# A two-layer decoder trunk: PE's instructions of both attentions tied to the order of the source

## The chip, the core and the metric

The kernel runs on one core of a Trainium2 chip. The metric is the time of one execution on the device in microseconds (us); of several executions the median is taken. Engines are named as in the profile: PE is TensorE (matmuls; PEld its weight loads), DVE is VectorE, ACT is ScalarE, POOL is GpSimd, SP is SyncE, whose queue issues nearly all DMAs.

## The reference

One sequence of 512 tokens, width 1024, float32. Two layers: a "forgetting" attention (FoX: 16 heads of 64, causal softmax with an added term from a running sum of log-sigmoid gates), then a latent attention (MLA: 8 heads, 128 plain and 64 rotary dimensions, keys and values from one shared compressed stream). Each is followed by an output projection, a residual and a squared-ReLU MLP with 4096 hidden units.

```python
def reference(x, ...):
    for layer in range(DEPTH):                      # DEPTH = 2
        h = rms_norm(x, norm_mix_g[layer])
        if layer < N_A_LAYERS:                      # layer 0
            x = x + fox_mixer(h, fox_w_in[layer], fox_b_f[layer], fox_w_out[layer])
        else:                                       # layer 1
            x = x + mla_mixer(h, ..., k_nope, k_rope, v_shared, cos, sin)
        x = x + sq_relu_mlp(rms_norm(x, norm_ffn_g[layer]), ffn_w_up[layer], ffn_w_down[layer])
        if layer == N_A_LAYERS - 1:
            k_nope, k_rope, v_shared = mla_shared_kv(x, ...)
    return rms_norm(x, final_norm_g)

# inside both mixers, for each block of 128 queries:
        logits = jnp.where(kpos[None, :] <= qpos[:, None], logits, -jnp.inf)
        p = jax.nn.softmax(logits, axis=-1).astype(v.dtype)
        return jnp.einsum('bhqk,bkhd->bqhd', p, v)
```

## The kernel before

Every product of float32 matrices is made of three matmuls on rounded operands: a tensor is split into a high half (ACT casts it) and a low half (DVE subtracts the high half from the source), and `three` issues high x high, high x low, low x high into one PSUM bank. Split tiles of 128 x 512 have the tag "r" (40 buffers). Weights arrive as pieces (tag "raw", two buffers; halves "whi" and "wlo", three buffers); a piece is loaded and split when the one before it is asked for. The weight pieces of the output projections numbered 3 and 4 go into "r" tiles instead.

**An attention** (`attention`, lines 378 to 412) runs over pairs of heads and, within a pair, over the four query blocks from the last (i = 3, 512 keys) to the first (i = 0, 128 keys). Step n of its loop does, in this order in the source:

1. `start(p)` on the first block of a pair: the filling is run until this pair's projections have been issued.
2. `scores` for both heads into two "sc" banks. In FoX that is six matmuls with a contraction of 64, alternating between the two heads, which lie in the upper and the lower 64 partitions. In MLA each head has three matmuls over 128, and then come six over 64, alternating.
3. `soft_step`: DVE adds the bias and takes the row's extreme, ACT takes the exponential, DVE normalizes.
4. For the block of three steps earlier (SKEW = 3): `turn` for each head. PE transposes the probabilities into a "tp" bank (three banks), ACT casts them to "pth" (high), DVE subtracts to "ptl" (low).
5. After a pair's last block, in between: `values` for each head (PE, from "pth" and "ptl" into a "tp" bank), and ACT and DVE combine the result to the context. In FoX ACT copies one half and DVE adds the other.
6. `fill.run`: a set number of matmuls of other work. In FoX it is 12 a step, and 18 more after the first head's values; in MLA 6 and 6. The work is a list of generators: in FoX the query and key projections of pairs 1 to 7 (24 matmuls each, "acc" banks) with two value projections, and then the first three columns of the output projection (`out_begin`), as far as contexts are there; in `out_begin` a context is split when first used (`ctx_part`). In MLA it is the query, key and value projections of later pairs, then the output projection. Two more columns, in the "sc" banks, are added as "out2" when the scores are over.

**What sets the order of instructions.** Each engine runs its instructions in the order of its stream, with semaphores between engines. The order within a stream is not the source's by itself: the scheduler of the kernel language plays the program through ahead of time, and lets an engine take, of the instructions that are ready in that play, the one written first. An instruction written earlier but not ready is passed. A tile waits for a free buffer of its tag.

The class `Engine` (lines 101 to 124) wraps PE, DVE, ACT and SP. While `order["on"]` is set, it adds from each instruction to the one before it on the same engine an edge without a semaphore, so that the stream keeps the order of the source. Before the change this is on only in the two MLP stages (`ffn`, lines 873 to 878), whose order is written out by hand as a list of steps: for PE, DVE and ACT, and for SP in the steps below 9. In both attentions the scheduler is free.

The pairs of FoX are numbered 0 to 7, its steps 0 to 31 and a tail of four without scores; pair p's first scores are in step 4p. Pair p's values come in step 4p + 7.

Of the kernel before, what the change touches and what calls it, by code (L numbers as in the profile page):

```python
# [95 lines left out]
@with_exitstack  # L96
def trunk(ctx: ExitStack, tc: tile.TileContext, xT, wts, gains, fing, rope, out):
    real = tc.nc
    order = {"on": False, "loads": False, "last": {}}

    class Engine:

# [4 lines left out]
        def __getattr__(self, op):  # L107
            fn = getattr(self.engine, op)

            def call(*args, **kw):  # L110
                ins = fn(*args, **kw)  # L111
                if order["on"] and (self.name != "sync" or order["loads"]):
                    before = order["last"].get(self.name)
                    if before is not None:
                        tc.add_manual_dep(
                            ins.ins,
                            before,
                            mybir.DependencyInfo(mybir.DependencyClass.NoSync, mybir.DependencyReason.DATA),
                            reason="as written",
                        )  # L120
                    order["last"][self.name] = ins.ins.name
                return ins

            return call

    class Core:
        tensor, vector, scalar, sync = (Engine(n) for n in ("tensor", "vector", "scalar", "sync"))
# [23 lines left out]
    def nm(s):  # L151
        uid[0] += 1
        return f"{s}{uid[0]}"
# [197 lines left out]
    def soft_step(scs, n, biases):  # L351
        m, rs, r = (small.tile([P, 2], F32, tag=f"sm{j}", name=nm("sm"), bufs=4) for j in range(3))
        Ls = [tt(), tt()]
        for e in range(2):

            nc.vector.tensor_tensor_reduce(
                out=Ls[e][:, :n], in0=scs[e][:, :n], in1=biases[e], scale=-1.0, scalar=3.4e38, op0=ALU.add, op1=ALU.min, accum_out=m[:, e : e + 1]
            )
        for e in range(2):
            nc.scalar.activation(  # L360
                out=Ls[e][:, :n], in_=Ls[e][:, :n], func=AF.Exp, scale=-1.0, bias=m[:, e : e + 1], accum_out=rs[:, e : e + 1]
            )
        nc.vector.reciprocal(r, rs)
        for e in range(2):
            nc.vector.tensor_scalar_mul(Ls[e][:, :n], Ls[e][:, :n], r[:, e : e + 1])
        return Ls

    def turn_unit(L, i, pth, ptl):

        n = (i + 1) * P  # L370
        tp = bank("tp")
        for j in range(i + 1):
            nc.tensor.transpose(tp[:, j * P : (j + 1) * P], L[:, j * P : (j + 1) * P], ident)
        src = tp[:, :n].rearrange("p (j q) -> p j q", q=P)
        nc.scalar.copy(pth[:, i : 4 * i + 1 : 3, :], src)
        nc.vector.tensor_tensor(ptl[:, i : 4 * i + 1 : 3, :], src, f32(pth[:, i : 4 * i + 1 : 3, :]), op=ALU.subtract)

    def attention(pairs, apool, start, scores, values, fill, per_step, out_gen):


        bufs = {}

        def turn(st, e):
            p, i, Ls = st
            if (p, e) not in bufs:
                bufs[p, e] = [apool.tile([P, 13, P], F32R, tag=t, name=nm(t), bufs=3) for t in ("pth", "ptl")]
            turn_unit(Ls[e], i, *bufs[p, e])

        steps = [(p, i) for p in range(pairs) for i in range(NB - 1, -1, -1)]
        ready = {}  # L390
        for n in range(len(steps) + SKEW + 1):
            if n < len(steps):
                p, i = steps[n]
                if i == NB - 1:
                    start(p)
                ready[n] = (p, i, soft_step(*scores(p, i)))
            elif n == len(steps):
                fill.add("out2", out_gen(["sc"] * 2))
            m = n - SKEW
            st = ready.pop(m, None)  # L400
            done = (m - 1) // NB if m > 0 and m % NB == 0 else None
            if done is not None:
                values(done, 0, *bufs.pop((done, 0)))
            if st:
                turn(st, 0)
            if done is not None:
                fill.run(per_step[1] if n < len(steps) else 6)
                values(done, 1, *bufs.pop((done, 1)))
            if st:
                turn(st, 1)  # L410
            if n < len(steps):
                fill.run(per_step[0])

    def out_begin(name, tags, outs, ready, part):

        mine = [(bank(t), blocks(piece(name))) for t in tags]
        outs += mine
        for ks in ((0, 2), (2, 4), (4, 6), (6, 7)):
            for pp, w in mine:
                for k in range(*ks):  # L420
                    while ready() <= k:
                        yield 1000
                    three(pp, *w[k], *part(k), k == 0, False)
                yield 3 * (ks[1] - ks[0])
# [3 lines left out]
    with ExitStack() as fx:  # L428
# [111 lines left out]
        def start(p):  # L540
            if p:
                fill.until(("qk", p))
            for q in (p, p + 1):
                if q < FH // 2 and q not in nbs:

                    nb = apool.tile([P, 2, S], F32, tag="nb", name=nm("nb"))
                    nc.sync.dma_start(nb, csc[2 * q : 2 * q + 2, :].partition_broadcast(P))
                    nbs[q] = nb

        def scores(p, i):  # L550
            n = (i + 1) * P
            q = slice(i * P, n)
            (qh, ql), (kh, kl) = qk[p]
            scs = [bank("sc"), bank("sc")]
            for a, b2, st, sp in ((qh, kh, True, False), (qh, kl, False, False), (ql, kh, False, True)):
                for e in range(2):
                    rows = slice(e * FHD, (e + 1) * FHD)
                    mm(scs[e][:, :n], a[rows, q], b2[rows, :n], start=st, stop=sp)
            nb = nbs[p]
            mask = maskz[:, S - P :].unsqueeze(1).to_broadcast([P, 2, P])  # L560
            nc.vector.tensor_tensor(nb[:, :, q], nb[:, :, q], mask, op=ALU.add)
            return scs, n, [nb[:, e, :n] for e in range(2)]

        def values(p, e, pth, ptl):
            if p >= 4:
                fill.until(("v4", 2 + (p - 4) // 2))
            if e == 0:
                ctxs.append(rt())
            cs = f32(ctxs[p])
            hd = 2 * p + e  # L570
            cx = bank("tp")
            for j in range(NB):
                w = v2[hd // 4, j][:, hd % 4].rearrange("p a d -> p (a d)")
                mm(cx[:, j * P :], w, pth[:, 4 * j : 3 * j + 4, :], start=j == 0, stop=False)
                mm(cx[:, j * P :], w, ptl[:, 4 * j : 3 * j + 4, :], start=False, stop=j == NB - 1)
            own = slice(e * FHD, (e + 1) * FHD)
            oth = slice((1 - e) * FHD, (2 - e) * FHD)
            nc.scalar.copy(cs[own], cx[oth])
            nc.vector.tensor_tensor(cs[own], cs[own], cx[own], op=ALU.add)
            whole[0] += e  # L580
# [21 lines left out]
        def out_gen(tags):  # L602
            return out_begin("fo", tags, outs, lambda: whole[0], ctx_part)

        fill.add("out", out_gen(["acc"] * 3))
        fill.run(12)
        attention(FH // 2, apool, start, scores, values, fill, FILL1, out_gen)
        fill.until("out2")
        split_ctx(FH // 2 - 1)
# [22 lines left out]
    def ffn(acc, layer, tokens, tail, begin):  # L632
# [8 lines left out]
        with ExitStack() as fs:  # L641
# [229 lines left out]
            begin(at)  # L871
            tail(len(seq), max(posted.values()), at, locals())
            for step in sorted(due):
                order["on"], order["loads"] = True, step < 9
                for _, _, fn, args in sorted(due[step], key=lambda d: d[:2]):
                    fn(*args)
            order["on"] = False
            order["last"].clear()
        state["next"] = first + [n for n, _ in PIECES].count(gname)

# [23 lines left out]
    def by_features(e, after, at, fn):  # L904
# [53 lines left out]
        for j, part in enumerate(("u2", "u3", "c11", "c21", "v", "c12", "u4", "c22")):  # L958
            for b in range(2):
                at(e + j // 2, 4, combine, b, part)  # L960

    ffn(acc, 0, ytok, by_features, put_away)
    for f in range(4, KD):
        close_feature(f)
# [11 lines left out]
    with ExitStack() as mx:  # L976
# [150 lines left out]
        cq = normed(q_t, rstd_tile(rs), "qa")  # L1127
        fill.until("q0")
        attention(MH // 2, apool, lambda p: fill.until(f"q{p}"), scores, values, fill, FILL2, out_gen)
        fill.until("out2")  # L1130

# [50 lines left out]
    def by_tokens(e, after, at, fn):  # L1182
# [44 lines left out]
        for j, part in enumerate(("u2", "u3", "c11", "c21", "v", "c12", "u4", "c22")):  # L1227
            for b in range(2):
                at(e + j // 2, 4, combine, b, part)

    ffn(acc, 1, xtok, by_tokens, turn_stream)
    psum["stack"].close()
    assert state["next"] == len(PIECES)
# [107 lines left out]
```

## Time and profile before

| | |
|---|---|
| median of 3 runs | 1143.74 us (1143.55 to 1149.49) |
| profiled execution, its own time | 1149.94 us |
| its span, first to last instruction | 1148.2 us |
| mean clock granted to PE | 0.99 |
| instructions | 14285, of these 5356 matmuls on PE |
| FoX attention, first scores to last values | about 52 to 234 us |
| MLA attention, first scores to last values | about 669 to 766 us |

A row in order of time reads: start, duration, engine, line, operation, output tile <- input tiles (buffer numbers left out), shape, count of instructions merged, and in brackets the idle time of the engine before it with what ended it. Every wrapped instruction has the line of the wrapper, L111, so rows are told apart by their tiles: "sc <- r" scores, "tp <- ident" turns, "tp <- pth, v" or "pth, r" values, "acc <- r, whi" projections. A merged row's duration runs to its last end; matmuls overlap in the records, so distances are taken from start to start. In the rows by stretches the columns are: from and to, length, then busy time and count of PE, PEld, DVE, ACT and POOL, then the clock granted to PE as a share of full speed, the DMA engines' share and GB/s.

### The profile page before, as it was taken

Reading aid. Unit: us, or ns where it says so; the run is one execution under the profiler, and the core shown is the slowest. Engines: PE = TensorE matmul, PEld = TensorE weight load, DVE = VectorE, ACT = ScalarE, POOL = GpSimd, SP = SyncE. Lnnn points to the kernel's source line nnn. Section 1 sums busy time; section 2 is a strip of 40 time slices with the busy share of each in tenths; the row PEclk is TensorE's granted clock in tenths of the full one; section 3 lists DMA queues with packets and bytes.
Section 4 is the critical chain, followed back from the end, with each engine's and each line's share of the span. In section 5 each row is a group of like instructions: output and inputs, shape, how many; then the busy total and the mean of one; then the engine's idle time right before and its main releaser. Section 6 shows DMA issues by size and latency. Waiting matters only on the chain.

```text
span 1148.2 us, 14285 instructions
## 1 busy us (share of the span) xinstructions
PE 1125.5 (98%) x5356; PEld 919.2 (80%) x5356; DVE 782.2 (68%) x1401; ACT 577.2 (50%) x1057; POOL 19.8 (2%) x83
## 2 busy tenths in 40 slices
PE   8999999999999999999999899999999999999996
PEld 6777887788888888888887768788888888888885
DVE  6797888863567676668793678846356666765785
ACT  5565655653664445434353456635555544444612
POOL 1000000001000000000000100000100000000000
PEclk9999999999999999999999889999999999999998
DMA  5322222142915215221343121222351522511301
GB/s 186 130 95 89 75 77 88 38 157 83 324 43 184 74 55 183 74 66 55 127 157 100 35 65 52 90 76 92 127 204 55 183 64 66 186 60 48 129 1 74
DMA packets 36822, 116.66 MB, mean 102 GB/s; under 512 B 4224, under 2 KB 4864, under 8 KB 36752
## 3 DMA queue, kind: packets, MB, share of 16 engines
q1 hardware_dynamic: 35888, 114.15, 29.9%
q10 hardware_dynamic: 864, 1.60, 0.4%
q8 instruction: 42, 0.69, 0.3%
q14 instruction: 28, 0.23, 0.1%
HBM read 109.40 MB, written 6.32 MB: 101 GB/s over the span
## 4 chain that ended last, share of the span: by engine, by line
PE 94%; DVE 2%; ACT 1%; DMA 1%; issue 1%; POOL 0%; ACTq 0%; SPq 0%
PE up L111 34%; PE acc L111 21%; PE go L111 17%; PE sc L111 8%; PE tp L111 7%; PE keep L111 6%; DVE r L111 1%; ACT t L111 1%; DVE fs L111 1%; DMA nb<-csc 0%; DMA t<-xT 0%; DVE wlo L111 0%; DVE t L111 0%; ACT whi L111 0%; ACT r L111 0%
## 5 line engine op out<-in xcount | busy, mean ns | idle before, releaser
L111 PE MATMUL acc<-r,whi 128*128 128x512 f32 x600 | 196.4, 408 | 5.4 <-ACT whi L111 4.9
L111 PE MATMUL up<-r,r 128*128 128x512 f32 x808 | 192.6, 390 | 0.0
L111 PEld LDWEIGHTS up<-r,r 128*128 128x128 f32 x808 | 151.2, 188 | 31.5
L111 PE MATMUL up<-r,whi 128*128 128x512 f32 x544 | 171.0, 391 | 0.0
L111 DVE TENSOR_TENSOR wlo<-raw,whi 128x1024 fp32r<-128x1024 f32 (+3 forms) x95 | 111.2, 1171 | 51.9 <-ACT whi L111 50.9
L111 DVE TENSOR_TENSOR t<-s,t 128x512 fp32r<-128x512 f32 x84 | 57.8, 688 | 121.8 <-ACT t L111 121.7
L111 ACT CAST whi<-raw 128x1024 fp32r<-128x1024 f32 (+3 forms) x95 | 95.5, 1008 | 88.2 <-PE acc L111 34.2
L111 PEld LDWEIGHTS acc<-r,whi 128*128 128x128 f32 x600 | 111.0, 192 | 31.6 <-ACT whi L111 4.9
L111 ACT ACTIVATE s<-up 128x512 f32<-128x512 f32 x56 | 33.4, 597 | 190.7 <-PE up L111 190.7
L111 PE MATMUL acc<-r,wlo 128*128 128x512 f32 x300 | 119.3, 398 | 0.0
L111 PEld LDWEIGHTS up<-r,whi 128*128 128x128 f32 x544 | 101.8, 188 | 21.0
L111 PE MATMUL up<-r,wlo 128*128 128x512 f32 x288 | 112.3, 390 | 0.0
L111 PE MATMUL go<-r,t 128*128 128x512 f32 x360 | 86.5, 389 | 0.0
L111 PE MATMUL sc<-r,r 128*128 128x512 f32 (+6 forms) x480 | 81.8, 360 | 2.1 <-ACT r L111 1.7
L111 PEld LDWEIGHTS go<-r,t 128*128 128x128 f32 x360 | 67.6, 188 | 14.0
L111 PE MATMUL go<-whi,t 128*128 128x512 f32 x240 | 78.8, 389 | 0.0
L111 PEld LDWEIGHTS sc<-r,r 64*128 64x128 f32 (+1 forms) x480 | 56.0, 188 | 26.1 <-issue 9.2
L111 ACT ACTIVATE t<-t,sm 128x512 f32<-128x512 f32 (+3 forms) x96 | 53.3, 557 | 36.7 <-DVE sm L111 36.5
L111 PEld LDWEIGHTS acc<-r,wlo 128*128 128x128 f32 x300 | 57.4, 191 | 12.9 <-issue 0.4
L111 PEld LDWEIGHTS up<-r,wlo 128*128 128x128 f32 x288 | 54.1, 188 | 11.5
L111 DVE TENSOR_TENSOR r<-raw,r 128x512 fp32r<-128x512 f32 x72 | 46.5, 684 | 22.1 <-ACT r L111 22.1
L111 DVE TENSOR_TENSOR r<-q,r 128x512 fp32r<-128x512 f32 x94 | 60.4, 683 | 0.0
(182 smaller groups left out, 1866.1 us busy)
## 6 DMA issues: line engine op xcount, KB each, us to landing
raw<-wts SPq DMA_DIRECT2D x122, 512.0 KB, 3.6
q<-wts SPq DMA_DIRECT2D x56, 512.0 KB, 4.6
nb<-csc SPq DMA_DIRECT2D x8, 512.0 KB, 4.7
t<-xT SPq DMA_DIRECT2D x8, 256.0 KB, 6.4
r<-xT SPq DMA_DIRECT2D x8, 256.0 KB, 6.3
xmid<-r SPq DMA_DIRECT2D x8, 256.0 KB, 7.3
r<-xmid SPq DMA_DIRECT2D x8, 256.0 KB, 4.2
xkeep<-r SPq DMA_DIRECT2D x8, 256.0 KB, 2.7
```

Source lines behind the costliest of these rows:

```text
L111: ins = fn(*args, **kw)
```

## The change

While the loop of an attention is issued, the wrapper now ties PE's instructions to the order of the source: scores, values and turns, and filling, as in the list above. `order["on"]` becomes a tuple of engine names instead of a flag. In the MLP stages the tuple names the engines that the flags named before. DVE, ACT, SP and POOL stay free in the attentions, and no instruction is added, removed or changed. The order begins with the first PE instruction of the loop and ends with its last; what lies before and behind is not tied to it.

```diff
-    order = {"on": False, "loads": False, "last": {}}
+    order = {"on": (), "last": {}}
...
                 ins = fn(*args, **kw)
-                if order["on"] and (self.name != "sync" or order["loads"]):
+                if self.name in order["on"]:
...
+        order["on"] = ("tensor",)
         steps = [(p, i) for p in range(pairs) for i in range(NB - 1, -1, -1)]
         ready = {}
         for n in range(len(steps) + SKEW + 1):
...
             if n < len(steps):
                 fill.run(per_step[0])
+        order["on"] = ()
+        order["last"].clear()
...
             for step in sorted(due):
-                order["on"], order["loads"] = True, step < 9
+                order["on"] = ("tensor", "vector", "scalar") + ("sync",) * (step < 9)
                 for _, _, fn, args in sorted(due[step], key=lambda d: d[:2]):
                     fn(*args)
-            order["on"] = False
+            order["on"] = ()
             order["last"].clear()
```

## The prediction

> **What bounds the kernel now.** I read the page's first part and its chain, then the busy time by stretches, then TensorE (PE), ScalarE (ACT) and VectorE (DVE) in order of time at the places where PE's order in the trace leaves the order of the source.
>
> ```profile
> PE 1125.5 (98%) x5356; PEld 919.2 (80%) x5356; DVE 782.2 (68%) x1401; ACT 577.2 (50%) x1057; POOL 19.8 (2%) x83
> PE 94%; DVE 2%; ACT 1%; DMA 1%; issue 1%; POOL 0%; ACTq 0%; SPq 0%
> ```
>
> ```profile
> 52.30:180.90 128.60, 128.60 (x792) 105.77 (x791) 105.60 (x291) 75.62 (x182) 0.00 (x0) 1.00 0.27 92
> 180.90:262.00 81.10, 79.60 (x401) 62.34 (x401) 61.77 (x139) 45.60 (x98) 0.00 (x0) 1.00 0.26 85
> ```
>
> PE is the bound: a microsecond that it loses ends up in the time. The first stretch is the first attention up to the scores of pair 6: PE is busy all of it (columns: length, busy time and count of PE, PEld, DVE, ACT, POOL, clock granted, DMA). A regular step there looks like this:
>
> ```profile
> 90.76 0.97 PE L111 MATMUL sc<-r,r 64*128 64x512 f32 x6
> 91.66 0.87 PE L111 MATMUL tp<-ident,t 128*128 128x128 f32 x6
> ...
> 94.45 0.62 PE L111 MATMUL acc<-r,whi 128*128 128x512 f32 x2
> 94.91 0.39 PE L111 MATMUL acc<-r,wlo 128*128 128x512 f32 x1
> 95.22 0.80 PE L111 MATMUL sc<-r,r 64*128 64x384 f32 x6
> ```
>
> Six score matmuls (three for each head), six turns, twelve of filling: exactly lines 391 to 412. The step takes 95.22 - 90.76 = 4.46 us, one filling matmul (94.91 - 94.45) / 2 = 0.23, and the one before a change of kind 0.31, so a change costs about 0.1. So the order asked for is already there, in 806 matmuls in a row by my walk through the loop. It is left only near 184, 201 to 216 and 225 to 232 us, and in the second attention, beyond a few single matmuls, near 737 to 745 and 759 to 766. There the old order put ready work into the time of a wait. The change's cost is what each wait is without that cover.
>
> **The change part by part.** No instruction is added or removed, and ACT, DVE, SP and POOL get no new order; their streams can only follow PE's. In the MLP stages the tuple names the same engines as the old flags, so nothing changes there: 0. In the 806 matmuls nothing moves: 0, and there is no cover to lose.
>
> *Place A, pair 6's first scores (step 24).* The source has only six filling matmuls between the last of pair 6's key projection and its scores.
>
> ```profile
> 184.10 0.38 PE L111 MATMUL tp<-ident,t 128*128 128x128 f32 x2
> 184.85 0.50 PE L111 MATMUL sc<-r,r 64*128 64x512 f32 x2 [0.36 <-ACT r L111]
> 186.33 0.73 PE L111 MATMUL sc<-r,r 64*128 64x512 f32 x4
> 189.48 0.79 PE L111 MATMUL sc<-r,r 64*128 64x384 f32 x6
> ```
>
> ```profile
> 184.18 0.62 ACT L111 CAST r<-t 128x512 fp32r<-128x512 f32 x1 [0.41 <-DVE t L111]
> ```
>
> ```profile
> 185.19 0.69 DVE L111 TENSOR_TENSOR r<-t,r 128x512 fp32r<-128x512 f32 x1
> ```
>
> The keys' high half is ready at 184.80 and the low half at 185.88. As written, PE runs the first score pair at 184.85, waits until about 185.95, runs two pairs (0.57), six turns (0.63) and the filling (2.93, the rest of the 4.46): next scores at 190.1 against 189.48, **+0.6**. The least is 4.46 + 0.1 from 184.10 without a wait, -0.8.
>
> *Place B, the turn to the output projection (steps 27, 28).* Behind the last projection matmul (200.89) the source has twelve matmuls of the output projection, then values, turn, twelve more, then pair 7's scores. The trace skips the twelve.
>
> ```profile
> 200.89 0.40 PE L111 MATMUL tp<-pth,v 128*128 128x512 f32 x1
> 206.00 0.44 PE L111 MATMUL tp<-ident,t 128*128 128x128 f32 x2 [0.90 <-DVE ptl L111]
> 207.20 0.78 PE L111 MATMUL sc<-r,r 64*128 64x384 f32 x3
> 215.64 0.79 PE L111 MATMUL sc<-r,r 64*128 64x384 f32 x3
> ```
>
> ```profile
> 203.07 0.62 ACT L111 CAST r<-raw 128x512 fp32r<-128x512 f32 x1
> 205.51 0.62 ACT L111 CAST r<-r 128x512 fp32r<-128x512 f32 x1
> ```
>
> ```profile
> 203.09 0.68 DVE L111 TENSOR_TENSOR r<-t,r 128x512 fp32r<-128x512 f32 x1
> 207.06 0.69 DVE L111 TENSOR_TENSOR r<-r,r 128x512 fp32r<-128x512 f32 x1
> ```
>
> The twelve need the splits of contexts 0 and 1 (r<-r). Those contexts are old, yet they are split only at 205.5: tiles tagged "r" come in written order here, the key's low half (DVE 203.09), then a weight piece in two halves (ACT 203.07 on), then the contexts. I take this order to stay. Without values and turn in between: key low half until 203.77, DVE's two weight halves until 205.15, ACT's first context cast from the second one's start, 204.46 to 205.08. PE waits 200.89 to 205.1 (4.2 us), and 0.5 more for the low halves (DVE at about 205.9 and 206.5). Behind it wait values, turn and pair 7's scores; their softmax has until pair 7's turns, some 10 us later, so nothing else becomes late. Against that stand the old order's idle 0.90, the heads' 384-column scores run apart (0.72 each time, where six together take 0.73), and ten changes of kind, 1.0: together 2.6. **+2.1**; least, if the splits come early, -2.6.
>
> *Place C, the last pair (steps 31 to 35).* Behind the values of pair 6 the source has nine output matmuls that need that very context, then six turns of pair 7 (twelve matmuls) in three buffers, then values.
>
> ```profile
> 225.31 1.03 PE L111 MATMUL tp<-ident,t 128*128 128x128 f32 x7
> 227.64 0.97 PE L111 MATMUL acc<-r,whi 128*128 128x512 f32 x3
> 233.67 1.29 PE L111 MATMUL sc<-r,r 128*128 128x512 f32 x4
> ```
>
> ```profile
> 225.51 0.58 ACT L111 COPY r<-tp 64x512 f32<-64x512 f32 x1 [0.49 <-PE tp L111]
> 226.96 0.63 ACT L111 CAST r<-r 128x512 fp32r<-128x512 f32 x1
> ```
>
> ```profile
> 226.12 0.69 DVE L111 TENSOR_TENSOR r<-r,tp 64x512 f32<-64x512 f32 x1 [0.37 <-ACT r L111]
> 227.91 0.68 DVE L111 TENSOR_TENSOR r<-r,r 128x512 fp32r<-128x512 f32 x1
> ```
>
> Copy, add, cast, subtract: the first of the nine can't start before about 227.5, the second before 228.2. As written PE idles from 225.7, where its four turns end, to 227.5 and again 0.6, and the nine end at 230.1. Three turns (0.8 us) fill the buffers; each next one waits for an ACT cast of about 0.5 and a DVE subtraction of 0.55 or less, so the last subtraction for head 0 ends near 233.3. Values (1.35), six score-bank matmuls (1.4) and values (1.35) end at 237.5, against 233.67 with the same work done: **+3.8**. The old order had put three of the turns and the six matmuls into the first wait. Without waits -0.4.
>
> *Place D, second attention, pair 3's first scores.* The third matmul needs a query half from DVE:
>
> ```profile
> 738.22 1.28 DVE L111 TENSOR_TENSOR r<-acc,r 128x512 fp32r<-128x512 f32 x2
> ```
>
> PE waits about 1.1 us to 738.9, then runs undivided pairs; the walk gives 746.7 against 747.06 at the next but one step: **-0.3** (bounds -1.4 with no wait, and +0.8 when the saving is absent).
>
> *Place E, its last turns.* Seven filling matmuls stood between the turns, the first and the last of them here:
>
> ```profile
> 759.61 0.70 PE L111 MATMUL acc<-r,whi 128*128 128x512 f32 x2
> 761.60 0.47 PE L111 MATMUL acc<-r,whi 128*128 128x512 f32 x1
> 761.92 0.47 PE L111 MATMUL tp<-pth,r 128*128 128x512 f32 x1
> ```
>
> Values can't start earlier (three buffers and DVE, as in C), so 7 x 0.23 = 1.6 comes behind, less some changes of kind: **+1.3** (0 to 1.6).
>
> Sum of the places: 0.6 + 2.1 + 3.8 - 0.3 + 1.3 = **+7.5 us**.
>
> **The clock.** Idle PE has a second price here.
>
> ```profile
> 640.49:650.73 10.24, 9.13 (x26) 7.50 (x27) 4.40 (x10) 2.56 (x5) 2.36 (x12) 0.50 0.00 1
> 667.80:671.21 3.41, 2.11 (x7) 1.07 (x7) 3.05 (x5) 3.31 (x7) 0.00 (x0) 1.00 0.35 115
> 671.21:678.04 6.83, 6.83 (x17) 4.42 (x16) 4.95 (x11) 2.65 (x7) 0.00 (x0) 0.50 0.29 77
> 203.59:207.00 3.41, 2.34 (x13) 1.28 (x12) 3.32 (x6) 3.01 (x8) 0.00 (x0) 1.00 0.52 159
> ```
>
> Behind a 3.41 us stretch in which PE was busy 62% the granted clock was 0.50 for 6.83 us; behind one with 69% it stayed at 1.00; the other fall lasted 10.24 us. At half clock 6.83 us do the work of 3.4, 10.24 that of 5.1. B has 4.2 us of no work at all; C has 2.4 idle in the 2.6 us from 225.7, and 2 more in the turns. I take a fall of the short kind at each, **+6.8**, and none at E (about 2 us idle, in short pieces): ends 0 and three long ones, 15.4. The Trainium skill, "TensorE: Matmul & The Clock Gate", section "HAM oscillation", warns of idle gaps over about 3.4 us. By that rule B falls and C does not; the trace speaks against it, for in the stretch of 62% PE was idle 1.3 us in all.
>
> Total +7.5 + 6.8 = +14.3 us. The profiled execution took 1149.94 (span 1148.2), which gives 1164.2; the median run is 6.2 us shorter, perhaps by a clock fall or two, and the same sum from 1143.74 gives **1158.0**.
>
> **The rivals.**
> 1. *Order pays, faster.* The splits of contexts 0 and 1 run early, in ACT's idle time before 201, and C, D and E find their operands: -0.8 - 2.6 - 0.4 - 1.4 - 0 = -5.2, 1138.5, a few less if the fall at 671 goes too. It decides at B: the first split would have to be there by 200.9 instead of 205.5. Against it: C's chain of four operations, 2.7 us long, which no order of other engines shortens. Chance 0.08.
> 2. *The stalls, but a clock that holds*: +7.5, 1151.2. For it: the 69% stretch. Chance 0.13.
> 3. *One fall, at the wait longer than a stretch (B)*: +10.9, 1154.6. For it: only there is a whole stretch empty. Chance 0.13. This is also what the skill's rule above makes of it.
> 4. *Three falls, or long ones*: up to 7.5 + 15.4 = +22.9, 1166.6. Chance 0.14.
> 5. *B's splits come early, the rest as forecast*: 0.6 - 2.6 + 3.8 - 0.3 + 1.3 = +2.8, 1146.5. Chance 0.09.
> 6. *The change does next to nothing*, since the trace is in the written order for most of both attentions and the rest is made up: 1143.7. Against it: no PE slack behind 262 us. Chance 0.07.
>
> **How the numbers follow.** The forecast itself has 0.36. A difference under 0.5% (5.7 us) is about what a measurement of this kernel can't tell from none. Slower: forecast and rivals 2 to 4, 0.76; same: 5, 6 and part of 1, 0.19; faster: the rest of 1, 0.05. The range runs from rival 5's lower side, 1145, to rival 4, 1167; the forecast's own is 1153 to 1163.
>
> **What the profile after would show.** PE's matmuls in written order throughout, sc x6 undivided; idle of PE before an "acc" released by an "r" of ACT or DVE of about 4 us near 201 and 2 us near 226; turns of the last pairs apart by DVE's "ptl"; clock 0.50 behind the first two. It is wrong if "r<-r" is cast before 201, if the clock stays at 1.00, or if PE's time grows where the order was the same before.

## The result and the profile after

The changed kernel took 1153.62 us (median of 4, 1153.27 to 1156.18) beside 1143.70 for the kernel before, a ratio of 1.0082 with the 95% interval 1.0056 to 1.0109. Measured once more, on the chip of some of the experiments, the ratio was 1.0045 (1.0025 to 1.0065). So it is slower: by 9.9 us in the first measurement and by 5.2 in the second, where 14.3 was forecast. The profiled execution took 1153.33 us.

The page of the kernel after, with busy time, granted clock and chain, and below it the clock row of the kernel before:

```profile
span 1151.5 us, 14282 instructions
...
PE 1121.2 (97%) x5356; PEld 917.6 (80%) x5356; DVE 782.4 (68%) x1401; ACT 577.1 (50%) x1057; POOL 20.1 (2%) x83
...
PEclk9999999899999999999999899999999999999998
...
PE 91%; DVE 4%; ACT 2%; DMA 1%; issue 1%; POOL 1%; SPq 0%; ACTq 0%; DVEq 0%
```

```profile
PEclk9999999999999999999999889999999999999998
```

PE's share of the chain fell from 94% to 91%, DVE's and ACT's rose: PE now waits for them. The clock row has three 8s, as it had before, but the first of them is new: it stands in the eighth of the 40 slices, near 206 us. The stretches of the first attention (columns as before):

```profile
52.30:181.20 128.90, 128.90 (x793) 105.99 (x792) 105.76 (x291) 75.72 (x182) 0.00 (x0) 1.00 0.29 93
181.20:271.00 89.80, 81.74 (x401) 64.37 (x400) 62.17 (x138) 45.59 (x98) 0.00 (x0) 0.96 0.24 77
202.52:205.93 3.41, 0.50 (x1) 0.19 (x1) 3.26 (x6) 3.41 (x8) 0.00 (x0) 1.00 0.14 20
205.93:212.76 6.83, 6.17 (x15) 4.97 (x16) 3.02 (x6) 1.12 (x3) 0.00 (x0) 0.50 0.45 146
229.82:233.24 3.42, 1.84 (x14) 1.51 (x12) 3.01 (x7) 2.55 (x5) 0.00 (x0) 1.00 0.00 0
```

The first row is what it was to 0.3 us: where the order had been the written one, nothing moved. The loss is in the second row, 89.80 us where the same work took 81.10. The third and fourth are place B, a stretch in which PE was busy only 15% and the clock at half behind it; the fifth is place C, where PE was busy 54% and the clock held.

To give each place its share I read the time between four points that both kernels pass with the same work done: the first scores of pair 5 (step 20), of step 26 and of step 31, and the first matmul of the MLP. Rows of PE in order of time, before and after (the first row of each is cut short by the view's window; all six score matmuls start there):

```profile
160.95 0.73 PE L111 MATMUL sc<-r,r 64*128 64x512 f32 x4
...
193.55 0.62 PE L111 MATMUL sc<-r,r 64*128 64x256 f32 x6
...
221.81 0.55 PE L111 MATMUL sc<-r,r 64*128 64x128 f32 x6
...
261.79 0.39 PE L111 MATMUL up<-r,whi 128*128 128x512 f32 x1
```

```profile
161.22 0.50 PE L111 MATMUL sc<-r,r 64*128 64x512 f32 x2
...
194.51 0.62 PE L111 MATMUL sc<-r,r 64*128 64x256 f32 x6
...
227.40 0.55 PE L111 MATMUL sc<-r,r 64*128 64x128 f32 x6
...
270.83 0.39 PE L111 MATMUL up<-r,whi 128*128 128x512 f32 x1
```

The differences are A 32.60 to 33.30 (+0.7), B 28.26 to 32.89 (+4.6), C 39.98 to 43.43 (+3.45), +8.8 in all. The same reading of each experiment's profile (us; the last column is the time at half clock in the first attention and its start):

| kernel | A | B | C | sum | half clock |
|---|---|---|---|---|---|
| before | 32.60 | 28.26 | 39.98 | 100.83 | none |
| after | 33.30 | 32.89 | 43.43 | 109.62 | 6.83 at 205.9 |
| after, again | 33.32 | 32.58 | 43.44 | 109.34 | 6.83 at 204.4 |
| B free | 33.32 | 28.26 | 44.76 | 106.34 | 3.41 at 229.9 |
| C free | 33.34 | 32.10 | 40.02 | 105.45 | 6.83 at 203.9 |
| B's wait filled | 33.36 | 30.04 | 43.44 | 106.84 | none |
| early split | 34.04 | 25.43 | 43.42 | 102.88 | none |
| early split, order free | 32.74 | 25.43 | 40.04 | 98.21 | none |
| tail rewritten | 33.17 | 32.83 | 41.93 | 107.93 | 6.83 at 204.3 |
| early split, 18 ahead, tail rewritten | 31.71 | 24.26 | 42.30 | 98.27 | none |
| the same, cover first | 31.71 | 24.26 | 40.47 | 96.45 | none |
| early split, 18 ahead, order free | 31.71 | 24.26 | 40.74 | 96.71 | none |
| cover first alone | 33.29 | 31.38 | 40.47 | 105.13 | 3.41 at 205.6 |
| tie kept behind the second loop | 33.58 | 31.66 | 43.42 | 108.65 | 3.41 at 207.7 |

In the three rows of kernels with 18 filling matmuls ahead of the loop ("the same, cover first" is one) the first point does not have the same work behind it as in the others: twelve more matmuls of 128x256 are done ahead of it, 1.4 us by the distance of their starts (0.12 us each). A has as much work as elsewhere there, B has 1.4 us less. For a comparison with the other rows their B is about 25.7 and their sums are 99.7, 97.9 and 98.1.

Where the clock holds, these lengths repeat to about 0.4 us at A and to a few hundredths at B and C. Whole times do not: all these profiles have between 3.41 and 17.07 us at half clock where the second attention begins (634 to 690 us), whatever the kernel. The profiled execution of before had 17.07 there and that of after 6.83, which accounts for these two lying only 3.4 us apart. The expectations below count C from the sixth matmul of step 31's scores, which is 0.28 later than the point used here (0.62 in the runs with 18 ahead).

What PE waits for in the kernel after:

```profile
PE acc L111 <- ACT r L111: 7.1, 4, 3.0
...
PE sc L111 <- ACT r L111: 1.8, 2, 1.2
PE sc L111 <- DVE r L111: 1.7, 3, 0.9
PE acc L111 <- DVE r L111: 1.3, 2, 1.1
PE tp L111 <- DVE ptl L111: 0.6, 1, 0.6
PE tp L111 <- ACT pth L111: 0.3, 1, 0.3
```

Each place is in it: A and D as "sc" for an r of DVE (0.59 and 0.90; at A behind 0.63 for an r of ACT, 0.36 before), B as "acc" for ACT's r (3.0) and DVE's (1.1), C as "acc" for ACT's r (1.6) and the turns' ptl and pth. B and C in the rows of PE and ACT:

```profile
201.63 0.40 PE L111 MATMUL acc<-r,wlo 128*128 128x512 f32 x1
205.02 0.50 PE L111 MATMUL acc<-r,whi 128*128 128x512 f32 x1 [3.00 <-ACT r L111]
206.59 0.80 PE L111 MATMUL acc<-r,whi 128*128 128x512 f32 x1 [1.07 <-DVE r L111]
...
230.91 0.63 PE L111 MATMUL tp<-ident,t 128*128 128x128 f32 x4
233.11 0.50 PE L111 MATMUL acc<-r,whi 128*128 128x512 f32 x1 [1.58 <-ACT r L111]
...
235.80 1.04 PE L111 MATMUL tp<-ident,t 128*128 128x128 f32 x8
237.45 1.12 PE L111 MATMUL tp<-ident,t 128*128 128x128 f32 x4 [0.61 <-DVE ptl L111]
...
238.90 0.47 PE L111 MATMUL tp<-pth,v 128*128 128x512 f32 x1 [0.33 <-ACT pth L111]
```

```profile
203.32 1.13 ACT L111 CAST r<-raw 128x512 fp32r<-128x512 f32 x2
204.36 2.69 ACT L111 CAST r<-r 128x512 fp32r<-128x512 f32 x5
```

At B the contexts are cast (r<-r) only behind the weight piece (r<-raw), from 204.36 on, and PE's first output matmul starts when the first cast is through. At C the output matmuls that need the new context stand first and nothing is beside them.

### The profile page after: what moved, and what is told of

Same layout as the page of the kernel before. It is cut to its first block, busy times and chain, and to the rows that moved or that the text cites. A ratio compares the mean times of both kernels' runs of the same rounds, so it can differ in the third digit from the quotient of the medians.

```text
span 1151.5 us, 14282 instructions
## 1 busy us (share of the span) xinstructions
PE 1121.2 (97%) x5356; PEld 917.6 (80%) x5356; DVE 782.4 (68%) x1401; ACT 577.1 (50%) x1057; POOL 20.1 (2%) x83
## 4 chain that ended last, share of the span: by engine, by line
PE 91%; DVE 4%; ACT 2%; DMA 1%; issue 1%; POOL 1%; SPq 0%; ACTq 0%; DVEq 0%
PE up L111 34%; PE acc L111 19%; PE go L111 17%; PE sc L111 8%; PE tp L111 8%; PE keep L111 6%; DVE r L111 1%; ACT t L111 1%; DVE wlo L111 1%; DVE fs L111 1%; DVE t L111 1%; DMA t<-xT 1%; DMA nb<-csc 0%; DMA raw<-wts 0%; ACT whi L111 0%
## 5 line engine op out<-in xcount | busy, mean ns | idle before, releaser
L111 PE MATMUL sc<-r,r 128*128 128x512 f32 (+6 forms) x480 | 76.5, 354 | 3.6 <-ACT r L111 1.8
L111 PEld LDWEIGHTS sc<-r,r 64*128 64x128 f32 (+1 forms) x480 | 54.6, 187 | 25.7 <-issue 7.1
```

## The experiments

**Giving back one place at a time.** In the first run PE's tie was lifted in the loop's steps 27 to 30, in the second from step 31 on:

```
         for n in range(len(steps) + SKEW + 1):
+            order["on"] = ("tensor",) if pairs == MH // 2 or not 27 <= n <= 30 else ()
```

> The changed kernel with PE's order left free in steps 27 to 30 of the first attention (place B) and kept everywhere else. Theory (B's wait is a term of its own: the trace put 4.6 us at B, 3.1 of them the clock's fall behind it): the time comes back by about 4.6, to some 1149, and the granted clock does not fall near 206 us; places A and C keep their +0.7 and +3.6. Rival (the slots that B loses are only moved: what goes early at B is missing as cover at C, or the reverse): less than 2 us come back, near 1152, and C grows by the rest.

> The changed kernel with PE's order left free from step 31 of the first attention on (place C), kept before it and in the second attention. Theory: C's 3.6 us come back, time about 1150, B as before with its wait of 3.0 us for an r of ACT and its clock fall. Rival (the loss at C is B's: B has put the output projection's matmuls ahead, and the filling that the old order had for C is used up): C still loses 2 us or more, time 1152 or above. Places B and C together: with both theories right, this run and the one with B freed lie 4.6 and 3.6 below the changed kernel.

They took 1.0026 (1.0015 to 1.0038) and 1.0033 (1.0020 to 1.0045) of the time before, that is +3.0 and +3.8 us. With B free, B has the 28.26 of before to the hundredth, and with C free C has 40.02; the other places do not move, but for the clock (with C free B is 32.10, with its fall). So on the path the losses are separate terms. One thing came otherwise: with B free the clock fell at C.

```profile
226.46:229.87 3.41, 1.61 (x8) 0.96 (x7) 2.23 (x4) 1.73 (x3) 0.00 (x0) 1.00 0.00 0
229.87:233.28 3.41, 3.41 (x13) 2.79 (x12) 0.00 (x0) 0.31 (x1) 0.00 (x0) 0.51 0.00 0
```

The stretch of C's wait was 47% busy here, and 3.41 us at half clock followed, which is C's 44.76 instead of 43.43. Of the six profiles with C as written this is the only one in which it fell. With D's 0.2 taken off, the two paths give +5.3 and +4.4; without the fall at C the first would be +4.0, inside its interval (+1.7 to +4.4).

**The price of the clock.** Thirteen matmuls, whose product nobody uses, were put where B's wait begins:

```
+        if name == "fo" and len(tags) == 3:
+            busy = bank("tp")
+            for _ in range(13):
+                mm(busy, h[0][0][:, :P], h[1][0], start=True, stop=True)
```

> The changed kernel with 13 matmuls of 128x512 put into B's wait, into a bank that nobody reads (their product is left unused; the output is the same). Theory (a good part of B is the clock, which falls because PE does nothing for 3 us): PE is busy through the wait, the clock stays at 1.00 behind 206 us, and B costs about +1.5 instead of +4.6: time about 1150.5. Rival 1 (the wait itself is the price): no change or up to 1 us slower, 1153.5 to 1155, since the added matmuls take PE's time. Rival 2 (a fall that is due anyway, merely moved): another fall turns up within the next 30 us, and the time is 1153 to 1154.

```profile
201.45 3.12 PE L111 MATMUL tp<-r,r 128*128 128x512 f32 x13
204.61 0.49 PE L111 MATMUL acc<-r,whi 128*128 128x512 f32 x1
206.19 0.50 PE L111 MATMUL acc<-r,whi 128*128 128x512 f32 x1 [1.08 <-DVE r L111]
```

```profile
202.52:205.93 3.41, 2.55 (x11) 1.54 (x9) 3.41 (x5) 3.41 (x7) 0.00 (x0) 1.00 0.30 84
205.93:209.35 3.42, 3.16 (x14) 2.64 (x15) 2.61 (x5) 0.71 (x2) 0.00 (x0) 1.00 0.82 214
```

The useful matmuls start when they did, the clock stays at 1.00, and B takes 30.04 instead of 32.89. So B's +4.6 is +1.8 of order and +2.85 of clock. The run took 1.0047 (1.0034 to 1.0061), +5.4, with the path at +6.0. By the profile the theory held and both rivals fell: B is shorter, and no other fall came before 640 us. The whole times alone would not show it, for 1.0047 can't be told from the changed kernel's 1.0045.

**The changed kernel again**, beside other runs:

> The changed kernel itself once more, beside the kernel before on the same chip as the next three. Theory (the places' sum, measured from pair 5's scores to the end of the output projection: 109.62 - 100.83 = +8.8 with a clock fall at B, -0.2 in the second attention): +8.6, a ratio of 1.0075. Rival (the fall at B does not come in each execution): between +5.8 and +8.6, in two groups of times.

The ratio is the 1.0045 told above, +5.2 (2.9 to 7.4). In the profiled execution the fall at B was there, and the path gives +8.5; the theory's 1.0075 lies just above the interval. No profile shows whether the fall came in the other seven executions, so the rival is not refuted. The spread at the second attention's start is in both kernels' times. At the same mean clock, 0.994, nine executions of before had a mean span of 1143.3 and two of after 1148.4: so with as much time at half clock the order alone costs about 5.1. That is an estimate, since the mean clock is given to a thousandth, and a thousandth of 1148 us is 1.15; the places' sum without the clock is +5.75.

**Splitting the contexts early**, in the changed kernel and in the kernel before:

```
             whole[0] += e
+            if e and p < FH // 2 - 1:
+                split_ctx(p)
```

> The changed kernel with each context (but the last) split into its two halves as soon as both of its heads are in, not when the output projection first asks for it. Theory (B's wait exists only since contexts 0 and 1 are split at 202 us, behind the weight piece): the twelve output matmuls run at 201 without a wait, no clock fall; by the prediction's bound B is -2.6 instead of +4.6, so the time is about 1147. Rival (the splits need room among the tiles tagged r, and what holds them longer delays the key and query halves or weight pieces): new waits of sc or acc for an r between 60 and 200 us, time 1152 or more.

> The kernel before, PE's order free, with each context (but the last) split as soon as both heads are in. Theory (the order as written gains at B once the operands are there, because it saves the old order's idle 0.9, heads' scores run apart and changes of kind): without the order the early split brings at most the 0.9, so the time is 0 to -0.9 against before. Rival (the split alone is what counted, the free order then falls into the written one by itself): B comes out as -2.8 as in the changed kernel with early splits, without C's +3.4: 2.5 to 3 below before.

With the tie 1.0016 (1.0003 to 1.0029), +1.8; without it 0.9971 (0.9955 to 0.9987), 3.3 below before. B is 25.43 in both, 2.8 under before, where the bound said 2.6. So the operands were what B lacked: once they are there, the free order falls into the written one by itself (at B the two runs' 140 matmuls stand in the same order, one by one), and the theory that the order itself brings the gain was wrong. The tie then costs at A, 34.04 against 32.74. In the run with the tie:

```profile
184.49 0.50 PE L111 MATMUL sc<-r,r 64*128 64x512 f32 x2 [0.93 <-ACT r L111]
186.02 0.73 PE L111 MATMUL sc<-r,r 64*128 64x512 f32 x4 [1.03 <-DVE r L111]
```

**Rewriting the tail.** First the filling of step 31 was put behind the turns of step 32, and more behind later turns:

```
-            if n < len(steps):
+            if n < len(steps) - 1:                      # first attention only
                 fill.run(per_step[0])
+            elif len(steps) <= n < len(steps) + SKEW:
+                fill.run(9 if n == len(steps) else 6)
```

> The changed kernel, PE's order still as written, but the last pair's steps of the first attention written otherwise: the twelve filling matmuls of step 31, nine of which need the context just made, stand behind the turns of step 32, and six of the filling behind the turns of steps 33 and 34 each. Theory (C is lost only because of where the filling is written: the chain copy, add, cast, subtract of 2.7 us has nothing beside it): C's 3.46 come back, and up to 0.5 more; time 5 to 5.5 above before, B's clock fall unchanged. Rival (what limits C is the turns' three buffers and DVE's subtractions, which a moved filling does not shorten): less than 1.5 come back, and new waits for ptl of DVE appear between the turns.

> The changed kernel with the early split, the tail rewritten as in the run beside it, and 18 instead of 12 filling matmuls ahead of the loop, so that pair 6's scores have 12 matmuls of other work ahead of them instead of 6. Theory (places add up: A 0, B -2.8, C 0, D -0.2): 3 below before. Rival (A's 1.4 with early splits comes from the buffers tagged r, which the splits hold longer, not from the missing cover): A keeps 0.7 to 1.4, so 1.6 to 2.3 below before.

The first took 1.0047 (1.0030 to 1.0064); C fell by 1.5 only, to 41.93, less than half of what the theory had, and the rival's waits for ptl did not come either. The second took 0.9973 (0.9960 to 0.9985), 3.1 below before; A lost its cost altogether (31.71), so with early splits too A was a matter of cover and its rival fell. That the time is the theory's 3 below is luck: C kept 2.3 of its cost, and with the 1.4 of work done earlier the path shows 1.2 at these places and 0.2 at D. C's remainder shows in the tail's rows of the first:

```profile
231.01 0.55 PE L111 MATMUL tp<-ident,t 128*128 128x128 f32 x3 [0.52 <-DVE r L111]
231.80 0.51 PE L111 MATMUL acc<-r,whi 128*128 128x512 f32 x1 [0.23 <-ACT r L111]
233.37 0.50 PE L111 MATMUL acc<-r,whi 128*128 128x512 f32 x1 [1.07 <-DVE r L111]
```

The turns of step 32 are too short to cover the chain of the context. What came next put work in between that needs no context, as the free order had done: six matmuls of the second output group at the end of step 31, the nine behind step 32's turns, six more behind those of 33 and 34.

```
+            elif n == len(steps) - 1:
+                fill.gens.insert(0, ("out2", out_gen(["sc"] * 2)))
+                fill.run(6)
+                fill.gens.append(fill.gens.pop(0))
```

> As the run with early split, 18 filling matmuls ahead of the loop and the rewritten tail, but the tail once more another way: behind the last turn of step 31 stand six matmuls of the output projection's second group, which need no new context; the nine that need the context just made stand behind the turns of step 32; six more of the second group each behind the turns of steps 33 and 34. Theory (what was left of C in the first rewriting, 1.95 above the free order, is the wait of 1.07 and 0.23 for the context's halves and 0.52 for a bank, since nothing independent was written between the values and the nine): C falls from 41.65 to about 39.7, and the time is 4.5 below before. Rival (ACT's and DVE's queue of the turns' copies sets C, whatever stands between): C stays above 41 and the time is within 0.5 of the run with the first rewriting, 3 below before.

```profile
222.59 0.66 PE L111 MATMUL tp<-ident,t 128*128 128x128 f32 x4 [0.60 <-DVE r L111]
223.00 1.63 PE L111 MATMUL sc<-r,r 128*128 128x512 f32 x6
224.47 0.81 PE L111 MATMUL tp<-ident,t 128*128 128x128 f32 x6
225.04 0.77 PE L111 MATMUL acc<-r,whi 128*128 128x512 f32 x2
```

The waits of "acc" are gone, and C is 40.47, 0.5 above the free order; the theory holds. The kernel took 1141.48 us, 0.9949 (0.9931 to 0.9968) of the time before: faster than both kernels, by 5.8 (3.7 to 7.9) against before. Of this the path shows 3.0 (97.9 against 100.8) and 0.2 at D; the rest is not shown to be the change's. The second rewriting alone, in the changed kernel:

> The changed kernel with the second rewriting of the tail alone (six independent matmuls first, then the nine behind step 32's turns). Theory: A +0.7 and B +4.6 with its clock fall stay, C is 39.7 instead of 43.16; from pair 5's scores to the end of the output projection about 106.2. Rival: C 41.5 or more, 108.

C was 40.47 here too, and the sum 105.13; the theory's 106.2 was too high because the fall at B was a short one, 3.41 us (B 1.5 shorter than in the kernel after), against which C came back by 2.96 where 3.46 was told.

**The same without the tie:**

> The kernel before with the early split and the 18 filling matmuls ahead of the loop, PE's order free. It has no tie: whatever it gains is not the order's. Theory (the free order reaches what the best written one reaches, but for D's 0.2): as the run beside it within 1 us, 3 to 4.5 below before. Rival (the written order is worth something once all its operands are there in time: undivided pairs, fewer changes of kind): 1 us or more slower than the run beside it.

It took 0.9986 (0.9972 to 0.9999), and so by the whole times the rival holds. By the path it does not: A and B are equal to the hundredth and their matmuls stand in the same order, C differs by 0.27, and D's 0.2 comes on top. Of its eleven executions besides the profiled one seven had a mean clock of 0.991, while four of the six of the run beside it had 0.994. At equal clock the spans go with the path: at 0.991 these seven are 2.9 below two executions of before (1143.8 against 1146.6), where the path has 2.7; at 0.994 the four are 4.0 below six of before (1139.6 against 1143.7), where it has 3.2. Why the clock fell more often without the tie is not settled.

**Place E.** The tie was kept through the filling behind the second attention's loop:

```
         fill.until("out2")
+        order["on"] = ()        # moved here from the end of attention
+        order["last"].clear()
```

> The changed kernel, but with PE's order in the second attention kept through the filling that stands behind its loop. Theory (place E's cost did not come because that filling is not tied and still goes between the last turns): from the last scores of the second attention to the first matmul of its MLP 50.5 to 51.1 us, where both kernels have 49.46; that is the +1.3 of the prediction (0 to 1.6). Rival (the turns' wait would be filled or absent anyway): 49.5.

The stretch took 51.10 where it is 49.46 otherwise, +1.64. First the kernel after, then this one:

```profile
762.14 1.04 PE L111 MATMUL tp<-ident,t 128*128 128x128 f32 x8
762.93 0.71 PE L111 MATMUL acc<-r,whi 128*128 128x512 f32 x2
...
764.88 0.27 PE L111 MATMUL tp<-ident,t 128*128 128x128 f32 x1
764.91 0.48 PE L111 MATMUL acc<-r,whi 128*128 128x512 f32 x1
765.24 0.47 PE L111 MATMUL tp<-pth,r 128*128 128x512 f32 x1
```

```profile
766.98 1.03 PE L111 MATMUL tp<-ident,t 128*128 128x128 f32 x8
768.63 1.12 PE L111 MATMUL tp<-ident,t 128*128 128x128 f32 x4 [0.62 <-DVE ptl L111]
770.08 0.47 PE L111 MATMUL tp<-pth,r 128*128 128x512 f32 x1 [0.33 <-ACT pth L111]
```

## Why the prediction was right, and where it was not

The direction, the places and their mechanisms came as forecast, and 1153.6 lies within 1145 to 1167, in the forecast's own part of it (1153 to 1163), at its lower edge. The centre, 1158.0, was 4.4 too high.

- *No change in 806 matmuls*: right, 128.60 and 128.90 us for the stretch.
- *A, +0.6*: +0.7, with the wait for the low half (0.59) as told.
- *B, +2.1*: +1.8 without the clock (30.04 against 28.26). The waits were 3.00 and 1.07, 4.07 in all, where 4.2 and 0.5 were worked out: PE came there 0.96 later than in the kernel before (194.51 against 193.55 at step 26), and the first cast was through when it had been forecast, at 205.0, so by the rows A's delay took a part of B's wait away, which a sum of separate places leaves out. That the order of the casts would stay was the assumption, and it did; the range's other end, -2.6, is the one that the early split reached, with -2.8.
- *C, +3.8*: +3.45. The chain of four operations cost 1.58 and 0.23 instead of 1.8 and 0.6, the idle time between the turns 0.94 instead of some 2.
- *D, -0.3*: -0.2: the stretch from pair 2's first scores to the MLP is 86.6 against 86.8, in every profile with the changed kernel's tie there (but for the run on place E, which is longer by E).
- *E, +1.3*: 0. This step failed. The filling between the last turns in the kernel before is not the loop's but that of the line behind it, where the tie is already off, so it went between the turns as before. With the tie kept on there the price came, +1.64. The prediction sized it rightly and overlooked which lines the tie covers.
- *The clock, two falls, +6.8*: one, +2.85. This is the term that was mis-sized most. At B it fell in all six profiles that have the wait (four times for 6.83 us, twice for 3.41), at C in one of six. The one that came was also cheaper than the 3.4 reckoned, since PE was idle in part of it anyway (6.17 busy of 6.83).

So +5.75 for the places and +2.85 for the clock, +8.6, where +7.5 and +6.8 were forecast. The errors do not cancel: E and the second fall, both of them costs that did not come, make up most of the difference, and the range was wide enough for it. With one fall, at B, the clock went as in rival 3, and its 1154.6 is nearer than the forecast. The reason given there does not carry it, though: it needs a whole empty stretch, and the wait was 3.00 and the stretch 15% busy. The Trainium skill, "TensorE: Matmul & The Clock Gate", section "HAM oscillation", names idle gaps over about 3.4 us; here the measurements go further than that rule: a wait of 3.00 and one of 1.07 with a single matmul between them brought a fall each time, and at C waits of 1.58 and 0.22 brought one once.

Of rival 1 the part that was testable came true elsewhere: with early splits the order pays at B. But the free order takes the same gain.

## What to carry to other kernels

An order that is written out by hand costs time where an instruction's operands are not there when its turn comes: 0.7, 1.8 and 3.45 us at A, B and C, while D gained 0.2 in spite of a wait. Before tying it, look where the free order already departs from it, for there lies work that covers a wait, and write that work into the place of the wait or bring the operand earlier. Here both together turned +8.6 on the path into -3.2, and -2.7 was reached without the tie. Where PE had nothing to do for 3 us and its clock fell for it, matmuls of the same length that nobody uses kept the clock and delayed nothing, in the one execution that was profiled.

## What the runs showed of the hardware

- Apart from the one that runs on to the kernel's end, the half-clock times come in lengths of 3.41, 6.83 and 10.24 us, and within one execution they start on one grid of 3.413 us; where that grid lies differs from one execution to the next (0.64 of a step in the profile of before, 0.33 in that of after). So the same wait can be cut by the grid in different ways, and at B, where the first wait is 2.99 or 3.00 us in all six profiles that have it, the fall behind it cost between 1.3 and 2.9 us (31.38 to 32.89 against the 30.04 without a fall).
- How busy PE is in the stretch ahead does not decide alone: the clock fell behind 47% and, in the kernel before, behind 62%, and held behind 54% in the kernel after. Counted over the steps of the grid from 30 to 1100 us in all fourteen profiles, the clock fell behind 22 of the 23 in which PE was busy less than half, behind 7 of the 16 between 50% and 62%, and behind none above that. What decides between 50% and 62% is open.
